# TensorE's order written out by hand in a two-layer hybrid encoder, and its first projection in full fp32

## The chip, the cores and the metric

The kernel runs on one core of a Trainium2 chip. The metric is the device time of one execution in microseconds, the median of several runs; less is better. One more execution was recorded by the hardware profiler, and all rows below come from it. The engines are TensorE (PE, with its weight loads as PEld), VectorE (DVE), ScalarE (ACT), GpSimd (POOL) and SyncE (SP, which issues all DMAs here). Each works through its own queue in order and waits on semaphores.

## What is computed

Two layers of an encoder over 512 prompt frames and 8 x 16 sample frames of 1024 channels, cut to what matters here:

```
hn   = rms_norm(x);  proj = hn @ w_in            # 1024 -> 1536: u_a, g_a, u_b, q, k, v
a    = RG-LRU(conv(u_a)) * gelu(g_a)             # two gate matmuls, a scan over time
b    = S5(u_b): B u, a scan of a complex state, C s, glu   # constants from exp, sin, cos
c    = softmax(q k^T / 8, sinks) v               # sliding window, per 64-frame chunk
x    = x + concat(a, b, c) @ w_out
x    = x + square(relu(rms_norm(x) @ w_up)) @ w_down       # 1024 -> 4096 -> 1024
```

Everything is fp32 at the interface.

## The kernel before

The frames are held transposed, channels on partitions, in two groups g = 0, 1 of 320 columns (256 prompt frames, 64 sample frames). All large matrix products are made of units: a 1024 x 128 block of weights against the 320 columns. `product` (line 247) makes it as 24 matmuls: the weights are split by `wunit` into a rounded part `wh` (ScalarE, line 243) and a remainder `wl` (VectorE, line 244), the activations likewise, and for each of 8 blocks of 128 channels three fp32r matmuls are issued (lines 252 to 254). Four of the 8 blocks are called a half.

A layer is, per group: a projection of 12 units (`in_proj`), three mixers (`lru`, `s5`, `attention`), 8 units of `out_proj`, then the MLP in four chunks of 8 units up and 8 down. The mixers use small fp32 matmuls and transposes, with VectorE, ScalarE and GpSimd work between them: in `s5` transposes of the input (line 176), products with K["B"] (L720), a scan, products with K["M"] and K["C"] (L752, L754), transposes back and a gate (L778); in `attention` scores (L842, L884), a softmax (`soft`, lines 813 to 835, on VectorE, ScalarE and GpSimd), transposes of the probabilities (L176) and products with the values (L860, L905); in `lru` four gate matmuls (L662). The S5 constants of a layer are computed on the chip: `small_prep`, `lru_const` and `s5_small` run a chain of small VectorE instructions, `s5_const` then makes from `tab` the tile `Rp` (VectorE in layer 0), which TensorE transposes into K["B"] (tile names `s<-ident,tab`), and K["M"] (L484). `Norm` sums the squares of the channels on GpSimd (L288), TensorE adds them over partitions (L294), VectorE takes the root (L308 to L315) and TensorE spreads it over the partitions (L326). The first 20 matmuls (L999) keep TensorE busy while x arrives.

The order on every engine is made by the framework's scheduler when the program is built: it takes instructions in the order of the code as priorities and places each where its own estimate of the times says that it could start. So the small matmuls of the mixers stand between the main products wherever the scheduler expected them to be ready. The PSUM banks are 3 for main products (`mm`), 2 for attention and the gates (`att`), 2 for S5 (`s5`), 1 for the norms (`fin`).

Of the kernel before, what the change touches and what calls it, by code (L numbers as in the profile page):

```python
# [11 lines left out]
F32 = mybir.dt.float32  # L12
# [7 lines left out]
NG = 320  # L20
# [127 lines left out]
def encoder_kernel(ctx: ExitStack, tc: tile.TileContext, a, o):  # L148
# [99 lines left out]
    def product(w, m):  # L248
        pt = bank("mm")[:, 0:NG]
        for k in range(8):  # L250
            h, l = w[k // 4]
            mm(pt, lhsT=h[:, k % 4], rhs=m[:, k, 0], start=k == 0, stop=False)  # L252
            mm(pt, lhsT=h[:, k % 4], rhs=m[:, k, 1], start=False, stop=False)  # L253
            mm(pt, lhsT=l[:, k % 4], rhs=m[:, k, 0], start=False, stop=k == 7)  # L254
        return pt


    class Norm:
        def __init__(self, g, gain):
            self.g, self.gain = g, gain  # L260
            self.h = bigr() if gain is not None else None
            self.ss = tp.tile([128, NG], F32, tag="ss", name="ss", bufs=1)

        def scaled(self, k):
            x = xT[:, self.g, k]
            if self.gain is not None:
                c = self.gain(k)
                act(self.h[:, k, 0], x, AF.Copy, scale=c)  # L268
                V.scalar_tensor_tensor(self.h[:, k, 1], x, c, self.h[:, k, 0].bitcast(F32), OP.mult, OP.subtract)  # L269

        def square(self, k):
# [3 lines left out]
            else:  # L275
# [6 lines left out]
                if k == 7 and tail:  # L282
                    self.sums(sq, False, True)
                elif k == 7 or tail:
                    V.scalar_tensor_tensor(self.ss, self.ss, 1e-6 * DM / 128, sq, OP.add, OP.add)
                    self.sums(self.ss, True, not tail)
# [3 lines left out]
        def sums(self, v, start, stop):  # L290
            if start:
                self.bank = bank("fin")
            for i, t0 in enumerate((0, 128, 192)):
                mm(self.bank[:, 320 + i:321 + i], lhsT=v[:, t0:t0 + 128], rhs=ones, start=start and i == 0, stop=stop and i == 2)  # L294

# [22 lines left out]
        def finish(self):  # L318
            with tc.high_priority():
                return self.broadcast(self.rsqrt())  # L320
# [122 lines left out]
    def s5_const(L):  # L443
        e1, e2 = (V, G) if L == 0 else (G, G)
        K = {}
# [18 lines left out]
        cmul(e1, slot(0), None, pk(ar), pk(ais), slot(1), pk(r0), pk(tm))  # L464
        for q in range(2):
# [15 lines left out]
        M = K["M"]  # L481
        b = bank("s5")[:, 0:256].rearrange("p (k r c) -> p k r c", k=8, r=2)
# [43 lines left out]
        return K  # L526


    def layer_small(L):
        P = {}  # L530
# [7 lines left out]
        P["S5"] = s5_const(L)  # L538
        return P
# [13 lines left out]
    def in_alloc():  # L553
        q = Proj()
# [7 lines left out]
        return q  # L562

    def in_evac(L, P, g, q, kind, i, pt):
# [23 lines left out]
        elif kind == "v":  # L588
# [3 lines left out]
            b = bank3("mm" if g else "att", 2, 128)  # L592
            for j in range(2):
                transpose(b[:, j], vT[:, 128 * j:128 * j + 128])
            act(kvs[L]["vt"][:, 2 * g:2 * g + 2], b, AF.Copy)
            dma(o["vs"][L, g], q.vS)
            if g == 1:
                dma(o["vp"][L], kvs[L]["vt"][:, 3])
# [23 lines left out]
    def in_proj(L, P, g, norm, raws=None):  # L622
        if g == 0:
            kvs[L] = {"kT": cst.tile([128, 512], F32, tag="kT", name="kT"), "vt": cst.tile([128, 4, 128], F32, tag="vt", name="vt")}
        q = in_alloc()
# [3 lines left out]
        q.early = {"ua": 2, "ub": 2} if L == 0 and g == 0 else {"ua": 2}  # L629
        q.r = norm.finish()  # L630
        cs = tp.tile([128, 2, NG], F32, tag="cs", name="cs", bufs=1)
        q.cosr, q.sinr = cs[:, 0], cs[:, 1]
        dma(cs, a["rope"][g])
        for t in (q.cosr, q.sinr):
            G.tensor_tensor(t, t, q.r, OP.mult)
        for n, (kind, i) in enumerate(units):
            in_evac(L, P, g, q, kind, i, product(wunit(w_in[n], raws if n == 0 else None), norm.h))
        return q


    def lru(L, P, g, q, mix, c):
# [10 lines left out]
        for ct in range(2):  # L652
            xc, t_, i_ = x2[:, ct], t2[:, ct], i2[:, ct]
            act(xc, u[:, ct, 0:LP], AF.Identity, scale=col("conv_w", 8 * L + ct), bias=col("conv_b", 2 * L + ct))
            for j in range(1, 4):
                V.scalar_tensor_tensor(xc, u[:, ct, j:j + LP], col("conv_w", 8 * L + 2 * j + ct), xc, OP.mult, OP.add)

# [19 lines left out]
        for ct in range(2):  # L677
# [8 lines left out]
                        q.ga[:, :, 256:320].rearrange("p c (b t) -> p c b t", t=16), OP.mult)  # L686
        act(mix[:, 0:2, 0], ov, AF.Copy, scale=0.5)
# [5 lines left out]
    def s5(L, P, g, q, mix, c):  # L693
# [9 lines left out]
        for ct, gs in cts:  # L703
            u2 = c.at(640 * ct, 8, 4, 16, parts=80)
# [4 lines left out]
        for ct, gs in cts:  # L709
            u2 = c.at(640 * ct, 4, 128, parts=80)  # L710
# [4 lines left out]
        for ct, gs in cts:  # L715
            d, jz = D[:, gs], J[:, gs]
# [28 lines left out]
        for ct, gs in cts:  # L745
            d = D[:, gs]
# [3 lines left out]
            for k in range(4):  # L750
                for r, p in enumerate((slice(0, 64), slice(64, 128))):
                    mm(bs[r][:, k], lhsT=Us[p, ct, k], rhs=tc2(K["M"][p, 4 * ct + k]), start=True, stop=False)  # L752
                for r in range(2):
                    mm(bs[r][:, k], lhsT=d[:, 2 * k + r], rhs=tc2(K["C"][:, 8 * ct + 2 * k + r]), start=False, stop=True)  # L754
            for r, b in enumerate(bs):
                act(y2[:, :, :, 16 * r:16 * r + 16], b.rearrange("p k (t c) -> p t k c", c=16), AF.Copy)
            b = bank3("s5", 4, 80)
# [16 lines left out]
        sg = c.at(1280, 2, NG)  # L774
        for ct in range(2):
# [4 lines left out]
        V.scalar_tensor_tensor(sg, sg, 1.0, zz, OP.add, OP.mult)  # L780
        act(mix[:, 2:4, 0], sg, AF.Copy, scale=0.25)
# [5 lines left out]
    def attention(L, P, g, q, mix, c):  # L787

# [124 lines left out]
        own()  # L913
        sprobs()
        for hf in range(2):
            sturned(hf)
        for hf in range(2):
            svalues(hf)
# [148 lines left out]
```

## Time and profile before

| what | us |
|---|---|
| runs | 1443.25, 1441.01, 1439.99 (median 1441.01) |
| the profiled execution | 1439.95 |
| its span in the trace | 1437.8 |
| TensorE busy | 1391.3 (97%) |
| VectorE busy | 905.4 (63%) |
| ScalarE busy | 665.1 (46%) |
| GpSimd busy | 378.0 (26%) |

The span is the time from the first to the last recorded instruction. Matmuls overlap in the record (a main product's matmul lasts 313 ns in it, and the next one starts long before that), so a busy TensorE is not one at its pace; its pace has to be read from how many matmuls a stretch holds. An fp32 matmul of the mixers leaves two records, an fp32r matmul and a transpose one. A row of a timeline gives the start, the duration, the engine, line, operation, tiles, shapes, count, and in brackets how long the engine had been idle and what ended it.

### The profile page before, as it was taken

How to read it: one execution, taken by the hardware profiler on the slowest of the kernel's cores; microseconds unless marked ns; L12 is line 12 of the kernel's file. 1: busy time of each engine (PE TensorE's matmuls, PEld its weight loads, DVE VectorE, ACT ScalarE, POOL GpSimd, SP SyncE). 2: the span in 40 equal slices, each digit the busy share in tenths (PEclk: the TensorE clock that was granted, in tenths of full speed). 3: DMA queues.
4: the chain of work that ended last, by engine and by line, in shares of the span. 5: the costliest groups of instructions: out<-in, count | busy, mean ns of one | idle time of the engine just before them, and what ended most of it. 6: DMA issues, size and time to landing. Idle time of an engine off the chain costs nothing.

```text
span 1437.8 us, 25702 instructions
## 1 busy us (share of the span) xinstructions
PE 1391.3 (97%) x9536; PEld 1324.8 (92%) x9536; DVE 905.4 (63%) x1750; ACT 665.1 (46%) x1384; POOL 378.0 (26%) x566
## 2 busy tenths in 40 slices
PE   7699999999999999999999999999999999999997
PEld 7688687899999999999998898889999999999997
DVE  8999789756544344357678768865664434434564
ACT  7666565545432122135675667653543212313543
POOL 4757289211010001063234225320110100100111
PEclk9999899999999999999999999999999999999998
DMA  7232123344422222234432342234442222223452
GB/s 252 83 120 75 62 83 97 125 138 136 153 81 74 75 79 75 79 101 153 137 111 88 108 140 90 91 103 140 148 146 90 78 78 75 80 74 109 149 176 95
DMA packets 91389, 156.26 MB, mean 109 GB/s; under 512 B 14337, under 2 KB 18305, under 8 KB 91265
## 3 DMA queue, kind: packets, MB, share of 16 engines
q1 hardware_dynamic: 91264, 154.63, 32.7%
q8 instruction: 75, 1.23, 0.3%
q14 instruction: 50, 0.40, 0.1%
HBM read 151.02 MB, written 3.37 MB: 107 GB/s over the span
## 4 chain that ended last, share of the span: by engine, by line
PE 81%; DVE 10%; POOL 4%; issue 2%; ACT 2%; DMA 1%; DVEq 0%; SPq 0%; ACTq 0%; POOLq 0%
PE mm L254 24%; PE mm L252 24%; PE mm L253 24%; DVE wl L244 2%; PE att L884 1%; PE att L905 1%; PE att L176 1%; DVE bigf L738 1%; PE s L754 1%; PE s L752 1%; DVE bigr L269 1%; PE att L860 1%; POOL att L835 1%; PE fin L326 1%; PE s L176 0%
## 5 line engine op out<-in xcount | busy, mean ns | idle before, releaser
L254 PE MATMUL mm<-bigr,wl 128*128 128x320 f32 x2688 | 838.5, 313 | 19.4 <-DVE wl L244 19.2
L252 PE MATMUL mm<-bigr,wh 128*128 128x320 f32 x2688 | 838.5, 313 | 0.7 <-ACT wh L243 0.5
L253 PE MATMUL mm<-bigr,wh 128*128 128x320 f32 x2688 | 837.4, 312 | 0.8 <-DVE bigr L269 0.8
L243 ACT ACTIVATE wh<-raw 128x512 fp32r<-128x512 f32 x544 | 340.9, 631 | 487.3 <-PE mm L253 470.9
L254 PEld LDWEIGHTS mm<-bigr,wl 128*128 128x128 f32 x2688 | 507.9, 189 | 30.2 <-DVE wl L244 24.2
L252 PEld LDWEIGHTS mm<-bigr,wh 128*128 128x128 f32 x2688 | 507.8, 189 | 7.6 <-issue 5.0
L253 PEld LDWEIGHTS mm<-bigr,wh 128*128 128x128 f32 x2688 | 507.8, 189 | 6.5 <-issue 3.6
L244 DVE TENSOR_TENSOR wl<-raw,wh 128x512 fp32r<-128x512 f32 x544 | 399.2, 736 | 176.4 <-ACT wh L243 157.9
L156 POOL TENSOR_SCALAR bigr<-t 128x320 fp32r<-128x320 f32 x128 | 63.8, 499 | 574.9 <-ACT t L956 570.4
L938 DVE TENSOR_TENSOR xT<-xT,mm 128x320 f32<-128x320 f32 x160 | 77.9, 487 | 127.7 <-PE mm L254 127.5
L956 ACT ACTIVATE t<-t 128x320 f32<-128x320 f32 x128 | 60.0, 471 | 131.4 <-DVE t L955 127.0
L958 DVE TENSOR_TENSOR bigr<-t,bigr 128x320 fp32r<-128x320 f32 x128 | 68.9, 542 | 67.9 <-POOL bigr L156 67.8
L955 DVE SCALAR_TENSOR_TENSOR t<-mm,r 128x320 f32<-128x320 f32 x124 | 60.6, 489 | 80.9 <-PE mm L254 80.7
L288 POOL TENSOR_TENSOR ss<-ss,sq 128x320 f32<-128x320 f32 x58 | 58.6, 1010 | 176.8 <-ACT sq L281 170.6
L835 POOL TENSOR_SCALAR att<-att,st 128x192 f32<-128x192 f32 (+3 forms) x40 | 36.7, 927 | 77.3 <-ACT wh L243 41.3
L269 DVE SCALAR_TENSOR_TENSOR bigr<-xT,sm,bigr 128x320 fp32r<-128x320 f32 x64 | 39.7, 633 | 2.3 <-ACT bigr L268 2.2
L825 ACT ACTIVATE att<-att,st 128x192 f32<-128x192 f32 (+3 forms) x80 | 30.6, 394 | 22.1 <-DVE st L823 17.5
L268 ACT ACTIVATE bigr<-xT,sm 128x320 fp32r<-128x320 f32 x64 | 34.3, 559 | 8.6 <-DVE xT L938 6.5
L281 ACT ACTIVATE sq<-xT 128x320 f32<-128x320 f32 x66 | 30.4, 461 | 9.0 <-POOL ss L288 4.8
L604 POOL TENSOR_TENSOR sw<-sw,cs 128x320 f32<-128x320 f32 x20 | 20.3, 1015 | 37.7 <-ACT sw L603 32.4
L176 PE MATMUL att<-ident,att 128*128 128x128 f32 (+1 forms) x144 | 26.1, 282 | 3.6 <-POOL att L835 1.7
L176 PEld LDWEIGHTS att<-ident,att 128*128 128x128 f32 (+1 forms) x144 | 16.9, 136 | 8.1 <-POOL att L835 2.7
(289 smaller groups left out, 1043.3 us busy)
## 6 DMA issues: line engine op xcount, KB each, us to landing
raw<-w_up SPq DMA_DIRECT2D x192, 256.0 KB, 2.6
raw<-w_down SPq DMA_DIRECT2D x192, 256.0 KB, 2.6
raw<-w_in SPq DMA_DIRECT2D x96, 256.0 KB, 2.6
raw<-w_out SPq DMA_DIRECT2D x64, 256.0 KB, 2.6
xT<-x SPq DMA_DIRECT2D x8, 320.0 KB, 5.7
yT<-xT SPq DMA_DIRECT2D x8, 320.0 KB, 2.5
cs<-rope SPq DMA_DIRECT2D x4, 320.0 KB, 2.9
gg<-gg SPq DMA_DIRECT2D x2, 512.0 KB, 4.9
```

Of the source, the lines that this page charges most:

```text
L156: return G.tensor_scalar(out, in_, 1.0, 0.0, OP.mult, OP.add)
L176: PE.transpose(out, in_, ident[0:n, 0:n])
L243: act(h, raw, AF.Copy)
L244: tt(l, raw, h.bitcast(F32), OP.subtract)
L252: mm(pt, lhsT=h[:, k % 4], rhs=m[:, k, 0], start=k == 0, stop=False)
L253: mm(pt, lhsT=h[:, k % 4], rhs=m[:, k, 1], start=False, stop=False)
L254: mm(pt, lhsT=l[:, k % 4], rhs=m[:, k, 0], start=False, stop=k == 7)
L288: G.tensor_tensor(self.ss, self.ss, sq, OP.add)
L938: tt(xT[:, g, k], xT[:, g, k], pt, OP.add)
L955: V.scalar_tensor_tensor(t, pt, 0.0, norm.r, OP.max, OP.mult)
L956: act(t, t, AF.Square)
L958: tt(am[:, f, 1], t, am[:, f, 0].bitcast(F32), OP.subtract)
```

## The change

Of layer 0's first projection (group 0) the weights and activations are no longer split: each of its 12 units is 8 fp32 matmuls (line 271 of the changed kernel) straight from the loaded weights, half of which go into buffers of tag `wl`. The scaled input is one VectorE instruction per block instead of a ScalarE and a VectorE one.

TensorE's instructions are no longer placed by the scheduler but stand in the order of the code (`manual_schedule`). The code is therefore rewritten: a stage is a `stream` that yields after each half of a product, each mixer is a generator that yields after each step, `TURNS` sets the order of the 31 steps (L for lru, S for s5, A for attention), and `weave(steps, n, fill, m)` spreads m halves over n steps. The evacuation of a product is issued after the first half of the next one; the norm's sums (`flush`) and its spread (`finish`) stand after the first and second unit of the stage behind it. The steps of `s5_const` are yielded too. The other four engines are still ordered by the scheduler, which now works against this order.

```diff
-    def product(w, m):
-        pt = bank("mm")[:, 0:NG]
-        for k in range(8):
-            h, l = w[k // 4]
-            mm(pt, lhsT=h[:, k % 4], rhs=m[:, k, 0], start=k == 0, stop=False)
-            mm(pt, lhsT=h[:, k % 4], rhs=m[:, k, 1], start=False, stop=False)
-            mm(pt, lhsT=l[:, k % 4], rhs=m[:, k, 0], start=False, stop=k == 7)
-        return pt
...
+    def wfull(src, raws=None):
+
+        if raws:
+            return raws
+        l = wp.tile([128, 4, 128], F32R, tag="wl", name="wl", bufs=4).bitcast(F32)
+        h = wload(src, 0)
+        dma(l, src[:, 4:8])
+        return h, l
...
+        def half(self, pt, m, n):
+            for k in range(4 * n, 4 * n + 4):
+                if self.full:
+                    mm(pt, lhsT=self.w[n][:, k % 4], rhs=m[:, k], start=k == 0, stop=k == 7)
+                else:
+                    h, l = self.w[n]
+                    mm(pt, lhsT=h[:, k % 4], rhs=m[:, k, 0], start=k == 0, stop=False)
+                    mm(pt, lhsT=h[:, k % 4], rhs=m[:, k, 1], start=False, stop=False)
+                    mm(pt, lhsT=l[:, k % 4], rhs=m[:, k, 0], start=False, stop=k == 7)
...
+    def stream(items):
+
+
+        items = list(items)
+        units = [i for i in items if isinstance(i, Unit)]
+        wait, late = [], []
+
+        def clear(all_=False):
+            for f in late:
+                f()
+            late.clear()
+            while wait and (wait[0][0].norm is None or wait[0][0].norm.r is not None):
+                unit, evac, pt = wait.pop(0)
+                more = evac(pt)
+                if more is not None:
+                    late.append(more)
+
+        for it in items:
+            if not isinstance(it, Unit):
+                it()
+                continue
+            it.load()
+            n = units.index(it) + 1
+            if n < len(units):
+                units[n].load()
+            for m, evac in it.prods:
+                m = m() if callable(m) else m
+                pt = bank("mm")[:, 0:NG]
+                for half in range(2):
+                    it.half(pt, m, half)
+                    if half == 0:
+                        clear()
+                    yield
+                wait.append((it, evac, pt))
+            it.w = None
+        clear()
+        clear()
+        assert not wait
...
+    def weave(steps, n, fill, m):
+
+        done = 0
+        for i in range(n):
+            next(steps, None)
+            while done < (i + 1) * m // n:
+                next(fill, None)
+                done += 1
...
+            if self.full:
+                V.tensor_scalar(self.h[:, k], x, self.gain(k), None, OP.mult)
...
+        evac = lambda kind, i: lambda pt: in_evac(L, None, g, q, kind, i, pt)
+        items = [Unit(w_in[n], [(lambda: norm.h, evac(kind, i))], norm, norm.full, raws if n == 0 else None)
+                 for n, (kind, i) in enumerate(units)]
+        return [begin, items[0], norm.flush, items[1], factors] + items[2:]
...
+    TURNS = "LSSLSSSS" "LAAAAAAA" + 5 * "AAS"
...
+        G3 = {"L": lru(L, P, g, q, lambda: gens(0), c), "S": s5(L, P, g, q, lambda: gens(0), c),
+              "A": attention(L, P, g, q, lambda: gens(0), catt)}
+        for t in TURNS:
+            next(G3[t], None)
+            yield
+        for v in G3.values():
+            assert next(v, "end") == "end"
...
-    for n in (512, 384, 320, 256, 128):
-        for _ in range(4):
-            mm(warm[:, 0:n], lhsT=zr[:, 0:128], rhs=zr[:, 0:n], start=True, stop=True)
...
-    raws = first(0)
-    q0 = in_proj(0, None, 0, norms[0], raws)
-    dma(sm[:, 80:], a["sm"][:, 80:])
-    first(1)
-    small_prep()
-    s5_small(lru_const())
-    P = layer_small(0)
-    mix0 = mixers(0, P, 0, q0, setup[0])
-    for L in range(DEPTH):
-        last = L == DEPTH - 1
-        q1 = in_proj(L, P, 1, norms[1])
-        mix1 = mixers(L, P, 1, q1)
-        hm = {0: out_proj(L, 0, mix0)}
-        mlp(L, 0, (0,), hm, None)
-        hm[1] = out_proj(L, 1, mix1)
-        mlp(L, 0, (1,), hm, None)
-        mlp(L, 1, (0, 1), hm, None)
-        mlp(L, 2, (0, 1), hm, None)
-        nxt = (lambda g: Norm(g, None)) if last else (lambda g: Norm(g, n1(L + 1)))
-        if not last:
-            P = layer_small(L + 1)
-        norms = mlp(L, 3, (0,), hm, nxt)
-        if not last:
-            q0 = in_proj(L + 1, P, 0, norms[0])
...
+    ctx.enter_context(tc.manual_schedule(engines={mybir.EngineType.PE}))
...
+    for n in 8 * (512,) + 4 * (512, 384):
+        mm(warm[:, 0:n], lhsT=zr[:, 0:128], rhs=zr[:, 0:n], start=True, stop=True)
+    dma(sm[:, 0:80], a["sm"][:, 0:80])
+    raws = first(0)
+    P = {}
+    q, m = [Proj(), Proj()], [{}, {}]
+    A = stream(in_proj(0, 0, norms[0], q[0], raws))
+    weave(iter(()), 1, A, 4)
+    dma(sm[:, 80:], a["sm"][:, 80:])
+    first(1)
+    small_prep()
+    s5_small(lru_const())
+    small = layer_small(0, P)
+    next(small)
+    weave(small, 2, A, 10)
+    M = mixers(0, P, 0, q[0], m[0], setup[0])
+    weave(M, 8, A, 10)
+    run(A)
+    for L in range(DEPTH):
+        last = L == DEPTH - 1
+        A = stream(in_proj(L, 1, norms[1], q[1]))
+        weave(M, 23 if L == 0 else 8, A, 16)
+        run(M)
+        M = mixers(L, P, 1, q[1], m[1])
+        weave(M, 8, A, 8)
+        run(A)
+        hm = {}
+        F = stream(out_proj(L, 0, m[0], hm))
+        weave(M, 7, F, 16)
+        run(F)
+        F = stream(mlp(L, 0, (0,), hm, fresh=(0,)))
+        weave(M, 16, F, 28)
+        run(M, F)
...
+            small = layer_small(L + 1, P)
+            next(small)
+            weave(small, 2, F, 24)
+            run(F)
+            q, m = [Proj(), Proj()], [{}, {}]
+            A = stream(in_proj(L + 1, 0, norms[0], q[0]))
+            weave(iter(()), 1, A, 14)
+            M = mixers(L + 1, P, 0, q[0], m[0])
+            weave(M, 8, A, 10)
+            run(A)
+            F = stream(mlp(L, 3, (1,), hm, nxt, norms))
+            weave(M, 15, F, 32)
+            run(F)
```

Two places on TensorE are shown as they stand in its queue. The first is where the transposes of `Rp` (tile `tab`) stand, from which K["B"] of layer 0 is made. Before:

```order
L252 MATMUL mm<-bigr,wh 128x320
L253 MATMUL mm<-bigr,wh 128x320
L176 MATMUL s_918<-ident,tab 128x128 x4
L176 MATMUL s_924<-ident,tab 128x128 x4
L254 MATMUL mm<-bigr,wl 128x320
L252 MATMUL mm<-bigr,wh 128x320
L253 MATMUL mm<-bigr,wh 128x320
```

Ahead of them stand 403 matmuls of main products, that is, all 12 units of the first projection and almost five of the next one. The same transposes now, from the last warming matmul on (L374 are the norm's sums, L411 its spread, `raw` and `wl` the two halves of a unit's weights):

```order
L1156 MATMUL fin<-bigr 128x384
L271 MATMUL mm<-bigf,raw 128x320 x8
L374 MATMUL fin<-ones,ss 128x1 x3
L271 MATMUL mm<-bigf,raw 128x320 x4
L271 MATMUL mm<-bigf,wl 128x320 x4
L176 MATMUL s_386<-ident,tab 128x128 x4
L176 MATMUL s_392<-ident,tab 128x128 x4
L411 MATMUL fin<-ident,rsq 128x128 x2
L411 MATMUL fin<-ident,rsq 128x64
L271 MATMUL mm<-bigf,raw 128x320 x4
```

The transposes have moved forward past ten of the twelve units, and the norm's spread stands behind them. The second place is the first prompt scores of layer 0, group 0 (64x64), whose softmax must be finished before the transposes of its probabilities. Before:

```order
L720 MATMUL s_1108<-bigf,Bm 128x80 x4
L884 MATMUL att<-kT,q 64x64 x6
L720 MATMUL s_1109<-bigf,Bm 128x80 x4
L884 MATMUL att<-kT,q 64x64 x2
L254 MATMUL mm<-bigr,wl 128x320
L252 MATMUL mm<-bigr,wh 128x320
```

Behind the scores follow 60 matmuls of main products and 8 of K["B"] before the first transpose `att<-ident,att`. Now:

```order
L276 MATMUL mm<-bigr,wl 128x320
L994 MATMUL att<-kT,q 64x64 x8
L176 MATMUL att<-ident,att 128x128 x4
L411 MATMUL fin<-ident,rsq 128x128 x2
L411 MATMUL fin<-ident,rsq 128x64
L274 MATMUL mm<-bigr,wh 128x320
```

The transposes stand directly behind the scores, and the halves that stood between are spread over other turns.

## Rows read from the trace of the kernel before

**Rows 1.** Windows, line 252 alone (one of three matmuls): stretch, its length, PE busy, records.

```profile
0.00:200.00 200.00, 71.29 (x224) 43.17 (x224) 0.95 0.35 115
200.00:360.00 160.00, 85.25 (x270) 51.19 (x269) 0.98 0.37 120
240.00:320.00 80.00, 43.92 (x140) 26.13 (x139) 1.00 0.39 124
400.00:600.00 200.00, 140.45 (x455) 85.42 (x455) 1.00 0.23 75
640.00:980.00 340.00, 176.38 (x559) 106.21 (x560) 0.98 0.35 113
```

**Rows 2.** The same windows, all: PE, PEld, DVE, ACT, POOL busy (records), clock.

```profile
0.00:200.00 200.00, 173.53 (x1150) 148.58 (x1151) 181.22 (x426) 127.47 (x297) 114.34 (x156) 0.95 0.35 115
200.00:360.00 160.00, 155.70 (x1066) 142.37 (x1065) 115.86 (x215) 84.73 (x191) 68.86 (x93) 0.98 0.37 120
240.00:320.00 80.00, 80.00 (x560) 72.33 (x559) 55.15 (x116) 38.32 (x94) 21.98 (x30) 1.00 0.39 124
400.00:600.00 200.00, 200.00 (x1366) 200.00 (x1365) 82.69 (x146) 51.21 (x89) 14.76 (x32) 1.00 0.23 75
640.00:980.00 340.00, 333.25 (x2351) 305.97 (x2350) 255.48 (x481) 209.76 (x474) 119.07 (x163) 0.98 0.35 113
```

**Rows 3.** Timeline of TensorE from 60 to 130 us.

```profile
67.68 0.31 PE L252 MATMUL mm<-bigr,wh 128*128 128x320 f32 x1
67.83 0.31 PE L253 MATMUL mm<-bigr,wh 128*128 128x320 f32 x1
...
72.08 0.64 PE L254 MATMUL mm<-bigr,wl 128*128 128x320 f32 x1 [3.95 <-DVE wl L244]
72.52 0.47 PE L252 MATMUL mm<-bigr,wh 128*128 128x320 f32 x1
72.78 0.47 PE L253 MATMUL mm<-bigr,wh 128*128 128x320 f32 x1
...
97.92 1.09 PE L176 MATMUL s<-ident,tab 128*128 128x128 f32 x8
```

**Rows 4.** The chain of waits in order of time: start, us, what.

```profile
789.01 1.08 PE s L778 x4
```

**Rows 5.** VectorE by line and form: count, busy us, mean ns.

```profile
L244 DVE TENSOR_TENSOR wl<-raw,wh 128x512 fp32r<-128x512 f32 x544 | 399.2, 736 | 176.4 <-ACT wh L243 157.9 <-PE mm L253 9.6
L269 DVE SCALAR_TENSOR_TENSOR bigr<-xT,sm,bigr 128x320 fp32r<-128x320 f32 x64 | 39.7, 633 | 2.3 <-ACT bigr L268 2.2
L439 DVE TENSOR_TENSOR tab<-s5s,tab 128x256 f32<-128x256 f32 x3 | 1.2, 411 | 0.0
L352 DVE TENSOR_SCALAR bigf<-bigf 128x36 f32<-128x36 f32 x6 | 1.1, 179 | 0.0
```

**Rows 6.** Timeline of all engines, from 12 to 28 us.

```profile
12.71 0.84 DVE L335 TENSOR_SCALAR nskp<-sm 128x8 f32<-128x8 f32 x1
...
24.58 1.10 POOL L288 TENSOR_TENSOR ss<-ss,sq 128x320 f32<-128x320 f32 x1 [6.09 <-ACT ss L274]
24.86 0.87 DVE L351 TENSOR_TENSOR bigf<-bigf 128x36 f32<-128x36 f32 x1
...
25.71 0.47 ACT L281 ACTIVATE sq<-xT 128x320 f32<-128x320 f32 x1 [0.69 <-POOL ss L288]
25.77 0.18 DVE L352 TENSOR_SCALAR bigf<-bigf 128x36 f32<-128x36 f32 x1
25.86 0.16 DVE L312 SCALAR_TENSOR_TENSOR rsq<-rsq 128x3 f32<-128x3 f32 x1
...
27.40 0.47 ACT L281 ACTIVATE sq<-xT 128x320 f32<-128x320 f32 x1 [0.17 <-POOL ss L288]
```

**Rows 7.** Timeline of TensorE from 255 to 267 us, the attention's rows.

```profile
256.66 0.87 PE L884 MATMUL att<-kT,q 64*64 64x192 f32 x8
...
265.68 0.60 PE L176 MATMUL att<-ident,att 128*128 128x128 f32 x4
```

More of the change, by code (lines that the diff above doesn't have):

```diff
@@ new lines, in encoder_kernel, with __init__, load @@
+    class Unit:
+        def __init__(self, src, prods, norm=None, full=False, raws=None):
+            self.src, self.prods, self.norm, self.full, self.raws = src, prods, norm, full, raws
+            self.w = None
+        def load(self):
+            if self.w is None:
+                self.w = wfull(self.src, self.raws) if self.full else wunit(self.src, self.raws)
+        def half(self, pt, m, n):
[7 more added lines that the diff above has]
+                    mm(pt, lhsT=l[:, k % 4], rhs=m[:, k, 0], start=False, stop=k == 7)
@@ new lines, in run, with __init__ @@
+    def run(*gens):
+        for g in gens:
+            for _ in g:
+                pass
+    def weave(steps, n, fill, m):
[5 more added lines that the diff above has]
+                done += 1
+    class Norm:
+        def __init__(self, g, gain, full=False):
+            self.g, self.gain, self.full = g, gain, full
+            if full:
+                self.h = Carve(bigf()).at(0, 8, NG)
+            else:
+                self.h = bigr() if gain is not None else None
@@ L591, in in_evac, with turn @@
             gcopy(q.vS, vT[:, 256:320])
[L592 to L598, printed above, removed]
+            def turn():
+                b = bank3("mm" if g else "att", 2, 128)
+                for j in range(2):
+                    transpose(b[:, j], vT[:, 128 * j:128 * j + 128])
+                act(kvs[L]["vt"][:, 2 * g:2 * g + 2], b, AF.Copy)
+                dma(o["vs"][L, g], q.vS)
+                if g == 1:
+                    dma(o["vp"][L], kvs[L]["vt"][:, 3])
+            return turn
         else:
@@ L980, in first @@
     def first(g):
-        norms[g] = Norm(g, n1(0))
+        norms[g] = Norm(g, n1(0), full=g == 0)
         raws = []
@@ new lines, in encoder_kernel @@
+    q, m = [Proj(), Proj()], [{}, {}]
[26 more added lines that the diff above has]
+        run(M, F)
+        run(stream(out_proj(L, 1, m[1], hm)))
+        run(stream(mlp(L, 0, (1,), hm, fresh=(1,))))
+        run(stream(mlp(L, 1, (0, 1), hm)))
+        run(stream(mlp(L, 2, (0, 1), hm)))
+        nxt = (lambda g: Norm(g, None)) if last else (lambda g: Norm(g, n1(L + 1)))
+        norms = {}
+        F = stream(mlp(L, 3, (0,), hm, nxt, norms))
+        if last:
+            run(F)
+            end = [norms[0].flush, lambda: finals(0)]
+            items = mlp(L, 3, (1,), hm, nxt, norms)
+            items[3:3] = end[:1]
+            items[5:5] = end[1:]
+            run(stream(items))
+        else:
+            P = {}
+            small = layer_small(L + 1, P)
[10 more added lines that the diff above has]
+            weave(M, 15, F, 32)
+            run(F)
@@ L1046, in _build @@
+    norms[1].flush()
+    finals(1)
 def _build(arrays):
```

180 lines of the change are left out of this document (101 added, 79 removed).

## Prediction

> **What bounds the kernel now.** I read the windows first, with the counts of one matmul of each three, because busy time says little of TensorE here. Where nothing but main products runs, 400 to 600 us, TensorE issues 1366 records in 200 us, one each 0.1464 us, and waits for nothing [rows 1, 2]. The reader should take this as the pace of a main matmul; at full clock no order makes it less. From 240 to 320 us it does 3 x 140 = 420 of these (61.5 us) and 140 other records in the remaining 18.5 us, so a record of the mixers costs 0.132 us, the switching between kinds included [rows 1, 2].
>
> With these two prices each stretch shows what TensorE lost, to waiting and to half clock. 0 to 200 us: 672 main matmuls (98.4 us) and 478 others (63.1) leave 38.5 us. 200 to 360 us: 810 (118.6) and 256 (33.8) leave 7.6. 640 to 980 us, layer 1's mixers: 1677 (245.5) and 674 (89.0) leave 5.5 [rows 1, 2]. The rest, but for about 10 us at the tail, is at pace. So a new order can win back some 50 us at most, 38 of them in the first 200 us. There VectorE is busy 181.2 of 200 us [rows 2], and the timeline shows TensorE waiting for its `wl`, and behind a wait of 3.95 us matmuls that start 0.26 us apart, the half of the two clock levels, instead of 0.147 [rows 3]. The transposes of Rp, with which S5 begins, come only at 97.9 us [rows 3], with almost five units of the next projection issued before them: the scheduler filled TensorE while VectorE's chain of constants ran.
>
> **The change part by part.**
>
> Full fp32. 12 x 8 = 96 fp32 matmuls replace 288. Four records of the S5 gate, two fp32 matmuls of the same 320 columns, take 1.08 us [rows 4]: 0.54 each, 51.8 us in all, against 288 x 0.1464 = 42.2. TensorE pays +9.7 us. The Trainium skill (FP8 and Floating Point Precision, TensorE Precision Notes) says that true fp32 takes four passes through the array; four passes at 0.1464 would make 0.586 and +14.1 us. The row has two records of 0.27 in it, and the row decides; the gate has the same shape and type.
>
> In return VectorE loses 24 `wl` of 0.736 = 17.7 us and ScalarE the 24 `wh`; eight instructions of 0.633 for the activations become single-input ones, whose price lies between 0.179 and 0.633, so 0 to 3.6 us saved [rows 5]. This is worth time only where VectorE sets TensorE's start; that is what the next part is about.
>
> The first wait. TensorE now does unit 0, the norm's sums, unit 1, and then stands before Rp's transposes. The sums: the squares go by a pair of ScalarE and GpSimd that repeats every 1.69 us (25.71 to 27.40) [rows 6]; seven from about 5 us on, and a last addition, give 17. Unit 0 is done at about 13, so some 4 us are waited; unit 1 ends at 17.5 + 8 x 0.54 = 22. For Rp the order of VectorE has 149 instructions from `nskp` on, which starts when its DMA has landed, 12.7 us [rows 6]: 21 of 256 columns at 0.411 (8.6 us), 8 of 0.633 (5.1), 2 of about 0.5, and 118 small ones. If each small one may start 0.09 behind the one before, as 25.77 and 25.86 do, they take 10.6 and Rp is ready at 38 us; at their whole 0.179 (most wait for their predecessor) they take 21.1, and with eight meetings with GpSimd, where 0.18 becomes 0.87, it is 54 [rows 5, 6]. I take 45, the middle, since the chain interleaves two strands. TensorE thus waits 23 us, with nothing to issue: all other units stand behind. The units that hid this chain before are now behind it.
>
> From Rp to the state in which both groups' projections, all of the first mixers and eight turns of the second are issued, on TensorE alone:
> - 80 fp32 matmuls, 43.2; 80 small records at 0.132 and eight of the gates at 0.27, 12.8; half clock behind the long wait, 2: 45 to 103 us.
> - 23 turns with 16 halves: 192 main matmuls, 28.1; 258 records, 34.1, and 8 of the gate, 2.2; waits, below, 16; half clock, 4: to 187.
> - 8 halves and eight turns: 14.1 + 8.5: to 210 us.
>
> The waits are those for a softmax. In before, from the last scores (ending 257.5) to the first transpose (265.7) 8.2 us go by while main products run [rows 7]; I use 7.6, since VectorE has less other work. In the new order of this stage nothing stands between the first prompt scores and their transposes (7.6 waited), 12 main matmuls after the sample scores (1.8, so 5.8), and 4.9 us of work before the last chunk's (2.7); the other two have 7.8 us between them and cost nothing while the softmax keeps to 7.6, which is thin cover. Behind each waiting transpose stands all else on TensorE, main products too. Bound from below: nothing, if VectorE, now less loaded, and the copies are quicker; from above: all five at 12 us, 40 instead of 16.
>
> Before had reached 672 main matmuls at 200 us, in a state otherwise the same. That is 96 more than the new order's 576, worth 14.1 us, so it was where the new one is at 210 already at 186. Loss: 24 us, the 9.7 of fp32 within it.
>
> The rest. In layer 0's second mixer 24 and 36 main matmuls (3.5 and 5.3 us) cover the two tight softmaxes: 4.1 + 2.3 waited and 2 for the clock, against the 7.6 lost before: +1. Layer 1 has three covers of 24 and one of 36: 3 x 4.1 + 2.3 = 14.6 waited against 5.5: +9. From below, layer 1 may win its 5.5 back (-5). Norm's sums and spread have 12 to 24 main matmuls between them, longer than the eight VectorE instructions; SP's queue carries as many weight loads as before, and the rope tables, which it now sends behind x and the constants, are first wanted by the fifth unit, issued after 60 us; the other warming matmuls and the earlier issue of the first group's final norm move nothing on the path, since the tail still ends with group 1's. I cost these at nothing; without the cover each norm would cost about 2 us.
>
> Sum: 24 + 1 + 9 = +34 us on the profiled execution's 1439.95, 1474; the median of the runs is 1.1 us higher, so 1475.
>
> **The rivals.**
>
> VectorE was the bound, and its relief comes through: faster. For it: 181 of 200 us busy [rows 2] and TensorE's wait for `wl` [rows 3]. If VectorE's chain is done at the lower bound, 38 us, and what VectorE no longer does (17.7 + 3.6) shortens all that follows, softmaxes included (16 and 14.6 gone, with them 6 of half clock), then 34 - 7 - 16 - 6 - 15 = -10, and with the 5.5 us of layer 1 won back -15: 1425. Against it: TensorE does not wait for VectorE's throughput here but for one chain and for latencies. It decides from the point where Rp comes before 35 us and the softmax below 4. This is what the Trainium skill (Perfetto Trace Analysis, Identifying the Most-Contended Engine) would say, that the engine with the highest occupancy of a regime is the one to relieve. Chance 0.14.
>
> It comes out even: Rp at 38 us, half of the softmax waits, no half clock: 34 - 7 - 8 - 6 - 7 = +6, and the lower end of layer 1's other waits brings it to about 1441. Chance 0.05.
>
> The thin covers break: VectorE, ScalarE and GpSimd are ordered by estimates, and if a softmax takes 12 us instead of 7.6, each of the five of the first mixer costs 4.4 more (22) and the two tight ones of the other three as well (26): 1475 + 48 = 1523. For it: small VectorE instructions grow from 0.18 to 0.87 beside GpSimd [rows 6]. Against it: main products stay between most pairs. Chance 0.19.
>
> **How the numbers follow.** My forecast, 1475 us, has a chance of 0.62, with a range of its own of 1455 to 1495 (Rp between 38 and 54 us, the softmax waits by half either way). The range for 8 in 10 is 1430 to 1515: it takes in the even case and the upper part of the faster one, and most of the broken covers. What a measurement can tell from no change here is about 0.2%, 3 us. Faster by more: 0.14; within: 0.05; slower: 0.62 + 0.19 = 0.81.
>
> **What would show it.** Right: TensorE idle from about 22 us until `s<-ident,tab`, released by VectorE, at about 45; the fp32 matmuls 0.27 us a record; 576 main matmuls' worth of work (24 units) at 210 us; in each mixer a wait for GpSimd's or VectorE's scaling (`att`) in front of the transposes of the first scores. Wrong: the transposes of Rp before 35 us or no wait there; softmax waits under 3 us; more than 24 units issued at 200 us; layer 1's stretch losing no more than before.

## The result and the profile after

The changed kernel takes 1484.6 us (median of four runs, 1483.8 to 1489.4), the kernel before, run beside it, 1442.1 us: a ratio of 1.0303, 95% interval 1.0276 to 1.0329. It is slower by 42.5 us; 1475 was predicted, with 1430 to 1515 as the range.

The windows of the changed kernel come first, with the columns of [rows 2].

```profile
0.00:200.00 200.00, 145.32 (x821) 115.61 (x822) 130.30 (x364) 91.44 (x221) 82.25 (x142) 0.85 0.29 96
...
400.00:600.00 200.00, 200.00 (x1365) 200.00 (x1364) 89.91 (x156) 57.03 (x99) 14.88 (x33) 1.00 0.27 89
640.00:980.00 340.00, 312.86 (x2222) 297.19 (x2221) 237.85 (x434) 197.25 (x432) 122.48 (x193) 0.95 0.34 110
```

The row of 400 to 600 us matches its partner in [rows 2]: the pace is the same where only main products run. In the first 200 us VectorE does less, 130.3 us against 181.2, and TensorE less too, 145.3 against 173.5. Between 640 and 980 us TensorE is busy 20 us less than before.

The view of waits sums TensorE's idle time by what ended it (us in total, times, longest):

```profile
PE att L176 <- DVE att L945: 35.6, 6, 10.7
PE s L176 <- DVE tab L522: 27.2, 1, 27.2
PE att L952 <- issue: 10.3, 3, 5.5
PE att L176 <- POOL att L945: 5.2, 3, 2.4
PE att L1015 <- ACT att L935: 4.7, 3, 2.3
PE att L176 <- ACT bigf L760: 4.5, 1, 4.5
```

Two things stand out: one wait of 27.2 us for Rp, and nine waits, 40.8 us together, in front of the transposes of a softmax (L176) until VectorE or GpSimd has scaled it (L945). Line 952 holds the sample scores.

To place the loss I use the additions of a product to the residual, which every version does 160 times. The 64th ends layer 0's third MLP part, where only main products run; the 96th ends the first MLP part of group 0 in layer 1, by which all mixers are done. In the timeline of that line, cut off at each, the last figure is the start of the 64th or of the 96th. Before:

```profile
L938 DVE TENSOR_TENSOR xT<-xT,mm x64: 472/489/490, 189.0 to 622.2; 128x320 f32<-128x320 f32 x64
...
L938 DVE TENSOR_TENSOR xT<-xT,mm x96: 466/489/490, 189.0 to 999.7; 128x320 f32<-128x320 f32 x96
```

After:

```profile
L1075 DVE TENSOR_TENSOR xT<-xT,mm x64: 472/489/489, 221.7 to 659.2; 128x320 f32<-128x320 f32 x64
...
L1075 DVE TENSOR_TENSOR xT<-xT,mm x96: 472/488/489, 221.7 to 1049.1; 128x320 f32<-128x320 f32 x96
```

So layer 0 costs 37.0 us more, and from the 64th to the 96th addition (layer 1's projections and mixers, and the MLP parts around them) 389.9 instead of 377.5, 12.4 more. The profiled pair is thus 49.4 us apart there, and still at the 144th, the place in layer 1 that answers to the 64th (1311.1 and 1360.4). That is 7 more than the medians, because the profiled execution is the slowest of the four. A second profile of the same order (the softmax first, below) has 656.9 and 1044.9 at these places, 34.7 and 10.5 more than before.

### The profile page after: what moved, and what is told of

Same layout as the page of the kernel before. It is cut to its first block, busy times and chain, and to the rows that moved or that the text cites. A ratio compares the mean times of both kernels' runs of the same rounds, so it can differ in the third digit from the quotient of the medians.

```text
span 1487.6 us, 25403 instructions
## 1 busy us (share of the span) xinstructions
PE 1377.3 (93%) x9436; PEld 1315.2 (88%) x9436; DVE 881.3 (59%) x1726; ACT 653.7 (44%) x1348; POOL 356.0 (24%) x566
## 4 chain that ended last, share of the span: by engine, by line
PE 85%; POOL 5%; DVE 4%; ACT 2%; issue 2%; DMA 1%; SPq 0%; DVEq 0%; POOLq 0%; ACTq 0%
PE mm L274 25%; PE mm L275 25%; PE mm L276 25%; PE mm L271 3%; PE att L176 1%; PE att L1015 1%; PE fin L411 1%; PE att L994 1%; PE s L176 1%; PE s L858 1%; PE s L886 1%; PE att L970 1%; DVE wl L244 1%; PE fin L374 1%; DMA raw<-w_in 1%
## 5 line engine op out<-in xcount | busy, mean ns | idle before, releaser
L274 PE MATMUL mm<-bigr,wh 128*128 128x320 f32 x2592 | 822.4, 317 | 2.3 <-POOL bigr L156 2.3
L275 PE MATMUL mm<-bigr,wh 128*128 128x320 f32 x2592 | 808.4, 312 | 0.9 <-DVE bigr L1091 0.9
L276 PE MATMUL mm<-bigr,wl 128*128 128x320 f32 x2592 | 808.0, 312 | 0.0
L243 ACT ACTIVATE wh<-raw 128x512 fp32r<-128x512 f32 x520 | 327.2, 631 | 517.6 <-PE mm L275 484.6
L274 PEld LDWEIGHTS mm<-bigr,wh 128*128 128x128 f32 x2592 | 494.3, 191 | 15.8 <-issue 8.3
L275 PEld LDWEIGHTS mm<-bigr,wh 128*128 128x128 f32 x2592 | 494.4, 191 | 2.2 <-DVE bigr L1091 1.3
L276 PEld LDWEIGHTS mm<-bigr,wl 128*128 128x128 f32 x2592 | 493.8, 190 | 0.0
L244 DVE TENSOR_TENSOR wl<-raw,wh 128x512 fp32r<-128x512 f32 x520 | 375.7, 723 | 179.8 <-ACT wh L243 168.4
L156 POOL TENSOR_SCALAR bigr<-t 128x320 fp32r<-128x320 f32 x128 | 59.7, 467 | 662.9 <-ACT t L1089 662.9
L176 PE MATMUL att<-ident,att 128*128 128x128 f32 (+1 forms) x144 | 23.7, 301 | 40.9 <-DVE att L945 35.6
L176 PEld LDWEIGHTS att<-ident,att 128*128 128x128 f32 (+1 forms) x144 | 16.8, 143 | 44.9 <-issue 31.0
L945 POOL TENSOR_SCALAR att<-att,st 128x192 f32<-128x192 f32 (+3 forms) x40 | 33.0, 832 | 67.9 <-ACT wh L243 45.7
L935 ACT ACTIVATE att<-att,st 128x192 f32<-128x192 f32 (+3 forms) x80 | 30.6, 395 | 27.3 <-DVE st L933 20.9
L348 ACT ACTIVATE bigr<-xT,sm 128x320 fp32r<-128x320 f32 x56 | 30.6, 561 | 11.3 <-DVE xT L1075 9.1
L349 DVE SCALAR_TENSOR_TENSOR bigr<-xT,sm,bigr 128x320 fp32r<-128x320 f32 x56 | 34.0, 615 | 0.5 <-ACT bigr L348 0.3
```

The source lines that it names most:

```text
L156: return G.tensor_scalar(out, in_, 1.0, 0.0, OP.mult, OP.add)
L176: PE.transpose(out, in_, ident[0:n, 0:n])
L243: act(h, raw, AF.Copy)
L244: tt(l, raw, h.bitcast(F32), OP.subtract)
```

## The experiments

**Rp later.** Ten more halves (five fp32 units) are issued ahead of Rp's transposes.

```
     next(small)
-    weave(small, 2, A, 10)
+    weave(iter(()), 1, A, 10)
+    weave(small, 2, A, 2)
...
-    weave(M, 8, A, 10)
+    weave(M, 8, A, 8)
```

> The changed kernel with the transposes of Rp placed ten halves (five fp32 units) later, behind units 2 to 6 of the first projection; nothing else moves. Theory A (the first loss is the order: nothing may be issued while VectorE makes Rp): the idle time of 27 us before the transposes of Rp falls to under 6 us and the kernel gains 18 to 25 us, about 1462 us. Rival B (VectorE and ScalarE set the end of the first 210 us whatever TensorE does in between): the wait moves to a later place of the first mixers and the gain stays under 6 us, 1479 us or more.

1473.0 us (ratio to before 1.0218, 1.0195 to 1.0242): a gain of 11.6, between the two theories. The wait for Rp in this kernel:

```profile
PE s L176 <- DVE tab L522: 13.5, 1, 13.5
```

Half of the wait went. The other half stayed because Rp itself slid, as the timeline of TensorE shows:

```profile
59.36 0.90 PE L176 MATMUL s<-ident,tab 128*128 128x128 f32 x3 [13.52 <-DVE tab L522]
```

It was 52.44 in the changed kernel. The products now done early bring VectorE work of their own, which takes its place among Rp's instructions: lru's convolution (L750, 3.9 us) and the evacuations of k and v (L699 to L701 and L672, 1.6 us). Cover is not free where the engine that is waited for has to empty it.

**fp32 taken out of the written order.**

```
-        norms[g] = Norm(g, n1(0), full=g == 0)
+        norms[g] = Norm(g, n1(0), full=False)
```

> The changed kernel with the first projection of layer 0 split into three products again (full fp32 left out), the written order kept. Theory A (fp32 costs TensorE 9.7 us, and VectorE's relief is worth little because only the units ahead of Rp can delay its chain): between 10 us faster and 3 us slower than the changed kernel, 1475 to 1488 us. Rival C (VectorE's throughput is the bound of the first 200 us, so that its 17.7 us of wl count in full): 8 to 18 us slower, 1492 to 1503 us.

1488.0 us (1.0322, 1.0302 to 1.0341). A further run of the changed kernel's own order (below) gave 1487.6, so full fp32 is worth between nothing and 3 us here, at the edge of theory A; rival C falls. The timeline of the split form:

```profile
55.25 1.94 PE L176 MATMUL s<-ident,tab 128*128 128x128 f32 x8 [24.38 <-DVE tab L522]
...
129.62 0.66 PE L176 MATMUL att<-ident,att 128*128 128x128 f32 x2 [10.51 <-DVE att L945]
```

and the same places with fp32:

```profile
52.44 1.94 PE L176 MATMUL s<-ident,tab 128*128 128x128 f32 x8 [27.20 <-DVE tab L522]
...
71.59 2.32 PE L271 MATMUL mm<-bigf,raw 128*128 128x320 f32 x8
73.74 2.32 PE L271 MATMUL mm<-bigf,wl 128*128 128x320 f32 x8
...
106.03 2.32 PE L271 MATMUL mm<-bigf,wl 128*128 128x320 f32 x8
...
128.37 0.66 PE L176 MATMUL att<-ident,att 128*128 128x128 f32 x2 [6.56 <-DVE att L945]
```

The fp32 groups start 2.15 us apart, 0.27 a record, as priced from the gate. From Rp to the first softmax's transposes it is 75.9 us with fp32 and 74.4 without, though TensorE has 8 us less to do there: it waits 17.0 us on the way instead of 11.7, 10.5 instead of 6.6 of it at the end. And Rp itself comes 2.8 us later without fp32. The price lies beside a chain on the other engines.

**Covers dealt unevenly.** A function like weave takes the number of halves after each turn; the turns' order stays.

```
-        weave(M, 23 if L == 0 else 8, A, 16)
+        if L == 0:
+            spread(M, A, [1, 0, 5, 0, 0, 0, 3] + [0, 3, 0, 0, 0, 2, 0, 0, 0, 0, 2, 0, 0, 0, 0, 0])
...
-        weave(M, 7, F, 16)
+        spread(M, F, [1, 1, 7, 1, 0, 1, 5])
...
-            weave(M, 15, F, 32)
+            spread(M, F, [1, 1, 8, 2, 1, 1, 5, 2, 4, 1, 1, 1, 3, 1, 0])
```

> The changed kernel with the same order of turns, but with the halves of main products dealt unevenly: 3 to 8 of them right behind each turn with scores, fewer elsewhere (22 halves fewer stand behind the other turns). Theory A (a softmax takes 8 to 16 us and the even deal covers only 0 to 3.5 of it): the waits before the transposes of the scores fall from some 45 us over the four mixers to under 15 and the kernel gains 20 to 30 us, about 1460 us. Rival D (the latency of a softmax is set by VectorE's and ScalarE's queues, which are filled by the very main products of the cover): the waits stay, the gain is under 8 us, 1477 us or more.

1472.5 us (1.0213, 1.0192 to 1.0235): a gain of 12.1. The waits:

```profile
PE s L176 <- DVE tab L529: 29.9, 1, 29.9
PE att L176 <- DVE att L952: 6.8, 3, 4.1
PE att L176 <- POOL att L952: 5.1, 3, 4.6
PE fin L418 <- DVE rsq L407: 4.7, 2, 3.1
PE att L959 <- DVE att L928: 4.5, 1, 4.5
...
PE mm L276 <- DVE wl L244: 3.6, 5, 1.6
```

The softmax waits fell from 40.8 to 11.9 us (the lines are 7 higher here), as theory A has it. But the gain is 12, since other waits appeared, for a norm's factors, weights and the samples' own values.

**Both.** The two edits together.

> Rp's transposes ten halves later and the uneven covers together, the written order otherwise. Theory A (two separate losses): the two gains of 12 us add up, 1455 to 1464 us, some 15 to 20 us above the kernel before. Rival B (both reach the same end, which VectorE sets): 1468 to 1473 us, as either alone.

1465.2 us (1.0161, 1.0145 to 1.0176). At 19.4 of 23.7 us the gains nearly add, 1 us short of theory A's bound: two losses, with a little in common. 23 us above before still remain.

**The written order taken away.** TensorE is ordered by the scheduler, the rewritten code and fp32 stay.

```
-    ctx.enter_context(tc.manual_schedule(engines={mybir.EngineType.PE}))
```

> The changed kernel without the written order: the scheduler orders TensorE as in the kernel before, the rewritten code and the full fp32 stay. Theory A (the written order is the loss): its waits go, fp32's 9.7 us stay and VectorE's relief of 17.7 us may show: 1425 to 1452 us. Rival E (the rewriting itself, units as streams with loads one unit ahead and later norms, or fp32, is the loss): 1465 us or more.

1433.3 us (0.9943, 0.9921 to 0.9965): 51 us less than the changed kernel and 9 less than before. Its residual additions:

```profile
L1075 DVE TENSOR_TENSOR xT<-xT,mm x64: 473/487/490, 190.1 to 622.6; 128x320 f32<-128x320 f32 x64
...
L1075 DVE TENSOR_TENSOR xT<-xT,mm x96: 455/486/490, 190.1 to 991.3; 128x320 f32<-128x320 f32 x96
```

The 64th comes with that of before; the gain is in layer 1, 368.7 us instead of 377.5.

**The written order in one part only.** Here it begins behind the eighth turn of layer 0's first mixer; from there the order is the changed kernel's.

```
-    ctx.enter_context(tc.manual_schedule(engines={mybir.EngineType.PE}))
...
+    ctx.enter_context(tc.manual_schedule(engines={mybir.EngineType.PE}))
     for L in range(DEPTH):
```

> The changed kernel in which the scheduler orders TensorE up to the eighth turn of layer 0's first mixer, and the written order begins behind it (from there on it is the changed kernel's, row by row). Theory A (two losses: Rp in front of its cover in the first stretch, and the softmaxes in all four mixers): the waits for the scaled softmax stay at some 40 us, the wait for Rp goes, 1460 to 1472 us. Rival J (the first stretch is nearly all of the loss, what comes later is hidden): 1436 to 1450 us.

1462.8 us (1.0143, 1.0125 to 1.0161). And the other way round, until that mixer, both of layer 0's projections and the first eight turns of the second mixer are issued:

```
-    ctx.enter_context(tc.manual_schedule(engines={mybir.EngineType.PE}))
+    written = ExitStack()
+    written.enter_context(tc.manual_schedule(engines={mybir.EngineType.PE}))
...
+        if L == 0:
+            written.close()
         hm = {}
```

> The complement: the written order only until layer 0's first mixer and both of its projections are done, the scheduler's order for all the rest. Theory A: the loss of the first 210 us stays (24 to 30 us against the scheduled form of this code), that of layer 0's second mixer and of layer 1 goes: 1456 to 1466 us. Rival J: 1475 us or more.

1462.9 us (1.0147, 1.0127 to 1.0167). Both as theory A: with the later part alone the softmax waits stay at 39.2 us and Rp's falls to 1.3, with the early part alone Rp's stays at 29.9 and the softmax waits fall to 12.6. The residual additions of the first of these two:

```profile
L1075 DVE TENSOR_TENSOR xT<-xT,mm x64: 474/487/490, 195.0 to 632.3; 128x320 f32<-128x320 f32 x64
...
L1075 DVE TENSOR_TENSOR xT<-xT,mm x96: 473/487/490, 195.0 to 1021.9; 128x320 f32<-128x320 f32 x96
```

and of the second:

```profile
L1075 DVE TENSOR_TENSOR xT<-xT,mm x64: 457/488/490, 213.8 to 653.0; 128x320 f32<-128x320 f32 x64
...
L1075 DVE TENSOR_TENSOR xT<-xT,mm x96: 457/487/490, 213.8 to 1021.3; 128x320 f32<-128x320 f32 x96
```

Against the form without a written order (622.6, and 368.7 to the 96th) the early part alone costs 30.4 us by the 64th addition and nothing after it (368.3); the later part alone costs 9.7 by the 64th and 20.9 in layer 1 (389.6). The two come to 59 us by medians and the whole to 51. The first mixer's later turns and the projection beside them are written in both, so their loss may be counted twice; this was not taken apart.

**fp32 alone in the code before.** Norm and in_proj take the full form for layer 0's first group, all else is the kernel before.

```
...
+            pt = fullproduct(wfull(w_in[n], rw), norm.h) if norm.full else product(wunit(w_in[n], rw), norm.h)
...
```

> The kernel before with one part of the change alone: layer 0's first projection in full fp32, the scheduler's order and the old code kept. Theory A (fp32 takes 9.7 us of TensorE and gives VectorE back 17.7 us in a stretch in which it is busy 181 of 200 us, and the two cancel): 1437 to 1447 us. Rival F (the gain of the changed kernel under the scheduler's order, 9 us, comes from fp32): 1430 to 1436 us. Rival G (in an order that already hides VectorE's chain, fp32's price stands alone): 1449 to 1454 us.

1454.2 us (1.0088, 1.0074 to 1.0101), 12.4 us slower than the kernel before beside it: rival G, fp32's price and a little more.

**The rewriting alone.** Neither the written order nor fp32.

> The changed kernel without the written order and without full fp32: what is left of the change is the rewritten code alone (streams of units, later sums of the norms, other accumulation flags in S5). Theory A (the rewriting gains its 9 us in layer 1, and fp32 is neutral): 1428 to 1438 us. Rival F (fp32 is the gain): 1440 us or more.

1438.7 us (0.9972, 0.9962 to 0.9983). So the rewriting gains 3 us by itself, just outside theory A's range, and fp32 another 5.4 on top of it (4 by the ratios), while it loses 12.4 on the old code. Neither theory had this. The traces show where the difference sits: up to the 16th residual addition, the end of group 0's first MLP part in layer 0, fp32 takes TensorE's idle time on the old code from 30 to 29 us and its mean granted clock from 0.96 to 0.92, and on the rewritten code the idle time from 33 to 26 us and the clock from 0.94 to 0.96. Which part of the rewriting turns fp32's sign was not tried.

**The softmax first in the other queues.** The softmax and the own values' copies stand in a block of high priority.

```
...
+            with tc.high_priority():
+                soft([b[:, :, 0:144] for b in bs], p, sks[:, L:L + 1], nsks[:, L:L + 1], True)
...
```

> The changed kernel with TensorE's written order untouched, but with the softmax and the copies of the samples' own values put first in the queues of VectorE, ScalarE and GpSimd. Theory H (behind the scores the chain is late because VectorE and ScalarE work off other things first: 16 us where the chain alone needs about 8): the waits for the scaled softmax fall from 46 us to under 22, the kernel gains 15 to 25 us, 1460 to 1470 us. Rival I (the chain's own length is the wait, so that only more cover helps): the waits fall by less than 10 us, 1476 us or more.

1487.6 us (1.0318, 1.0304 to 1.0333). The edit left the order of instructions on TensorE, VectorE, ScalarE and GpSimd as it was, so this is a second run of the changed kernel and tells H from I not at all. A different order on VectorE was not tried.

**Hints to the scheduler.** No written order, but the code in the order of the version with both edits.

> The form without the written order, with its program code in the order of the two edits that helped the written one (Rp's transposes later, uneven covers), as hints to the scheduler. Theory A (the scheduler already places main products where TensorE would wait, by its own estimates): no difference by more than 5 us from 1433 us. Rival K (its choice follows the order of the code, so better covers win there as well): 1418 to 1428 us.

1434.7 us (0.9956, 0.9941 to 0.9972), the same as without the hints, as theory A has it. The two versions without a written order and with fp32 are the best of all, ahead of both kernels.

## Why the prediction was right, and where it was not

**The first wait: right.** TensorE stands from 25.2 us until Rp's transposes at 52.44 (predicted 22 and 45, with 38 to 54 as the bounds), released by VectorE. It was taken as 23 us and is 27.2. That it begins 3 us late comes from half clock ahead of it: the first eight records of unit 1 take 4.40 us from 17.73 on, 0.55 each, where 0.27 had been put down. The first projection ends at 108.3 (predicted 103).

**The state of 24 units and eight turns, 24 us: right in the sum, and in part by luck.** It was reckoned at 210 and comes with this row of the timeline:

```profile
211.84 1.28 PE L759 MATMUL att<-bigf,gg 128*128 128x332 f32 x4
```

Two terms were mis-sized and cancel. The first is waiting. Of the first mixer's waits, 16 in the sum, the trace has 6.6, 1.0 and 3.8 for a softmax, 4.5 for the tanh of the gates on ScalarE (L760) and 1.4 and 2.3 for exponentials, 19.6 together. With the longer first wait TensorE idles 55.8 us up to here, 9 more than the sum has, and it works at half clock for some 33 us, which cost 17 by the records above where 6 had been put down. (The upper bound of these waits, all five at 12 us, adds up to 38 and not to 40.)

The second is the price of a small record. A stretch of the changed kernel at full clock, all records and then line 274 alone, one of three main matmuls:

```profile
250.00:314.00 64.00, 63.88 (x531) 58.52 (x529) 47.23 (x97) 34.49 (x86) 32.83 (x44) 1.00 0.33 105
...
250.00:314.00 64.00, 33.32 (x103) 19.28 (x103) 1.00 0.33 105
```

Three times 103 main matmuls take 45.2 us of it, and the other 222 records 18.8: 0.085 each, not the 0.132 that the prediction had read from before [rows 1, 2] and carried over. On some 400 small records that is 19 us won, an estimate, about what the waits and the clock cost beyond the sum. In the written order more small matmuls of one kind follow one another, as the two listings of the scores show; how much of the gain is due to that, to the rewritten code or to another mix of records was not taken apart.

The 186 reckoned for before is wrong too, because it took the two states as equal but for main products. At 200 us the kernel before has 458 small records behind it (1150 less 672 and 20 warming ones [rows 2]), the changed one here 416: 912 less 288 main, 192 fp32 and 16 warming ones.

```profile
0.00:212.70 212.70, 156.86 (x912) 126.11 (x913) 139.79 (x380) 102.42 (x247) 87.24 (x147) 0.86 0.29 97
```

The 42 are worth 5.5 us at 0.132, so before was in this state at about 180.5, and the loss up to here is some 31 us where 24 was the term. The same balance can be drawn without these prices at the 16th residual addition, where both kernels have issued the same records but for fp32's and the warming ones. It comes at 310.0 us before (first row) and at 347.6 after (second row):

```profile
0.00:310.00 310.00, 279.23 (x1870) 241.15 (x1871) 265.00 (x579) 184.17 (x436) 175.40 (x237) 0.96 0.34 112
0.00:347.60 347.60, 273.38 (x1770) 233.26 (x1771) 238.03 (x555) 170.46 (x403) 156.56 (x237) 0.89 0.31 101
```

Up to there TensorE idles 30 us before and 74 after. With fp32's 9.7 that is some 53 us more, and more half clock besides (granted clock 0.89 against 0.96), but the changed kernel is only 37.6 us late: the written order also gives something back, which the prediction did not have.

**fp32's 9.7 us within these 24: wrong in its place.** Its price per matmul is exact, and VectorE is relieved as foreseen (130.3 us of the first 200, against 146.5 in the split form). But in this order taking it out gains nothing: the term had been counted on the path, and it lay beside the chain through VectorE. Without fp32 the work goes and about as much waiting comes in its place.

**Layer 0's second mixer, +1: the step that failed.** The 64th addition is 37.0 us late and the state before it some 31, so this term is about 6 (11 against the 186 as reckoned), and only because cheaper small records pay for a part of it again: the step had 6.4 us of waits, and the rows below are 16.2. The step said that 24 main products cover 3.5 us of a softmax's 7.6. The rows of TensorE:

```profile
224.37 0.71 PE L952 MATMUL att<-att,qS 64*64 64x144 f32 x8 [3.13 <-issue]
...
240.99 0.66 PE L176 MATMUL att<-ident,att 128*128 128x128 f32 x2 [10.65 <-DVE att L945]
244.07 0.69 PE L176 MATMUL att<-ident,att 128*128 128x128 f32 x2 [2.43 <-POOL att L945]
```

From the last scores at 225.0 to the first transposes it is 16 us. What VectorE did in between (the samples' softmax is L929, L931, L941 to L945):

```profile
228.57 0.45 DVE L929 TENSOR_REDUCE st<-att 128x2 f32<-128x288 f32 x1
...
229.73 1.27 DVE L768 SCALAR_TENSOR_TENSOR bigf<-bigf 128x664 f32<-128x664 f32 x1
230.93 0.45 DVE L929 TENSOR_REDUCE st<-att 128x2 f32<-128x288 f32 x1
231.29 2.10 DVE L244 TENSOR_TENSOR wl<-raw,wh 128x512 fp32r<-128x512 f32 x2
...
234.64 0.51 DVE L931 TENSOR_SCALAR st<-st,nsks 128x4 f32<-128x4 f32 x1
...
237.43 2.10 DVE L776 TENSOR_TENSOR_SCAN bigf<-bigf,coll 128x332 f32<-128x332 f32 x2 [1.68 <-POOL bigf L156]
239.44 0.75 DVE L941 TENSOR_TENSOR st<-st 128x4 f32<-128x4 f32 x1
240.23 0.18 DVE L942 RECIPROCAL st<-st 128x4 f32<-128x4 f32 x1
240.44 0.60 DVE L945 TENSOR_SCALAR att<-att,st 128x144 f32<-128x144 f32 x2
```

Seven instructions of 0.2 to 0.8 us stand among those of S5, the recurrence and the weights; on ScalarE a table load of 1.28 us precedes the first exponential. The 7.6 had been read from a prompt chunk [rows 7]. The same softmax of the sample scores takes 8.5 us in the first mixer, from 119.8 to the transposes at 128.37, and 16 here. The windows of the two stretches:

```profile
119.80:128.40 8.60, 2.04 (x15) 1.81 (x13) 7.17 (x15) 6.68 (x18) 4.05 (x13) 0.87 0.20 61
225.00:241.00 16.00, 5.35 (x27) 5.11 (x25) 14.25 (x23) 7.01 (x18) 15.07 (x22) 0.72 0.25 83
```

VectorE is busy 83% and 89%, GpSimd 47% and 94%. Which of the neighbours doubles the time was not tried. This is the rival of the thin covers, come true in one mixer and, with 11 us, in layer 1's sample scores. Longer covers, in the uneven version, did take these waits away.

**Layer 1, +9: measured 12.4.** Its softmax waits come to 16.5 us, near the 14.6 of the sum, but the term has three more pieces. The form without the written order is 8.8 faster there than before, in code whose cost I had put at nothing, so the order alone costs 20.9. Among its waits is one kind that the prediction did not have: TensorE stops within the sample scores, twice beside the one above (5.53 us before 787.24 and 1.68 before 935.19), until VectorE has copied the samples' own values. The timeline of VectorE for it:

```profile
786.31 0.83 DVE L921 COPY att<-att 16x256 f32<-16x256 f32 x2
```

The copies end at 787.14 and the scores go on at 787.24; the profile says "issue", and in the uneven version one such wait names VectorE's copy. The code says why: there are two `att` banks, the own values take one and the sample scores both, so the second scores need the bank that the copies empty. And half clock follows the longest of these waits: the granted clock is 0.50 from 787.3 to 791.6, from 799.3 to 805.3 and from 946.9 to 952.0. What the cheaper small records give back in this stretch was not reckoned by itself.

**The rivals.** VectorE as the bound falls for the written order. It is busy 51 us less in the first 200 us, of which some 16 are fp32's by the split form and the rest is work that comes later, and the kernel is slower. So the most occupied engine was not the one to relieve here. Under the scheduler's order it depends on the code: fp32, which relieves VectorE, lost 12.4 us on the old one and gained some 5 on the rewritten one. What decided is the order: with the scheduler's the same code and the same fp32 are faster than before. That an even end was unlikely held as well.

## What to carry to other kernels

An order written by hand has to put cover behind each producer by that producer's measured latency in the very neighbourhood where it will stand: the softmax of the sample scores took 8.5 us in one mixer and 16 in the next. A wait written in front of independent work holds all of that work back, so what needs the longest chain goes last, and the cover's own evacuations on the chain's engine count against it. Do not carry a price from one order to another: a small matmul's record cost 0.132 us scattered among main products and 0.085 in the written order, and this paid back part of the new waits. Price a change of an engine's work by the path, not by its occupancy: 9.7 us more on TensorE cost nothing where it stood waiting anyway, and 12.4 us under the scheduler's order on the old code. On the rewritten code it was a gain, so neither number holds beyond its order.

## What the runs showed of the hardware

A small VectorE instruction can last as long as the GpSimd instruction beside it. The 128x4 addition of a softmax (L941), at 797.27 us of the changed kernel:

```profile
797.27 1.28 DVE L941 TENSOR_TENSOR st<-st 128x4 f32<-128x4 f32 x1 [0.42 <-ACT st L937]
798.59 0.18 DVE L942 RECIPROCAL st<-st 128x4 f32<-128x4 f32 x1
```

and GpSimd at the same moment:

```profile
797.27 1.26 POOL L781 TENSOR_TENSOR bigf<-bigf,ga 128x512 f32<-128x512 f32 x1
```

They start together and end within 0.02 us of each other. The trace has 20 of these additions. The 17 with no GpSimd instruction beside them last 0.13 to 0.17 us, and the 3 with one last 0.38, 0.75 and 1.28 and end with it, within 0.03 us. So a softmax on the path can pay for what GpSimd does beside it.

The clock stayed at half for the first microseconds after the long wait and was back before the fp32 stretch was half done, as the windows of the changed kernel say (seventh column):

```profile
52.00:58.00 6.00, 5.57 (x19) 4.58 (x20) 0.87 (x2) 1.63 (x3) 3.19 (x6) 0.51 0.01 4
58.00:68.00 10.00, 10.00 (x41) 7.15 (x40) 3.10 (x6) 1.98 (x4) 4.60 (x13) 1.00 0.31 105
```

A record of the fp32 matmuls takes 0.55 us at half clock and 0.27 at full clock, so half of these 5.5 us, some 2.8 us, is what it cost there; 2 had been put down.
